# Sample sequences of an mLSTM: state products in bfloat16 parts on 32 columns each, state updates on 32 rows each, splits interleaved over states

## The chip, the core and the metric

The kernel runs on one core of a Trainium2 chip. TensorE multiplies matrices into PSUM, VectorE and ScalarE work on elements and move results out of PSUM, GpSimd does some element work and issues DMAs, SyncE (SP) issues most DMAs. Each engine works through its own instructions in order and waits on semaphores for the others. The metric is the device time of one execution in microseconds, the median of three runs.

## What is computed

One layer of a hybrid decoder: an input projection of 512 prompt tokens and 64 sample tokens (8 sequences of 8 tokens), an mLSTM with 4 heads of 256, a convolution module, an output projection and a layer norm. All is float32 to the tolerance of the reference. The change touches the samples in the mLSTM alone, which is, for each head and each of the 8 sequences with its own state C of 256 x 256 and n of 256:

```python
num = (w_inter[..., None] * jnp.einsum('bhtd,bhde->bhte', qc, C)
       + jnp.einsum('bhts,bhse->bhte', s, vc))
den = w_inter * jnp.einsum('bhtd,bhd->bht', qc, n) + jnp.sum(s, axis=-1)
h = num / jnp.maximum(jnp.abs(den), jnp.exp(-m_t))[..., None]
C_new = decay[..., None, None] * C + jnp.einsum('bhs,bhsd,bhse->bhde', ws, kc, vc)
```

## The kernel before

**Precision.** A float32 product is made of three products of parts: a value is split into hi (a rounded copy, by ScalarE) and lo (the rest, by VectorE), both float32r, and hi*hi + lo*hi + hi*lo is accumulated.

**The input projection** sets the pace. It has 64 column blocks; three are done first, the others are the stages of the loop over ORDER, from stage 4 on. A stage runs over 16 steps k (KT); a step is six matmuls L184, three pairs of 256 and 320 columns, into one of two PSUM tiles pp. The weights come in units of four steps: SP loads raw (two units each), `split` (L76) makes whi on ScalarE (L85) and wlo on VectorE (L86) and is called three units ahead (RING 4), so that whi of a unit waits until TensorE is done with the unit four before. At a stage's end `evac` moves pp out: for q, k, v two ScalarE passes; for o two sigmoid passes (L757) and a GpSimd product (L774); for zm two sigmoid passes, two VectorE passes (L763) and a GpSimd product (L778).

**All other work is placed beside it** by a table at the foot: `at(s, k, f, ...)` has f emitted right after step k of stage s. The order of emission is the order on each engine. For head h the sample work counts from o: stage 8, step 8 for head 0, and stage 6h+7, step 10 for the others (steps past 15 run on into the next stages). `at(o[0], o[1] + n, ...)` is n steps after that. Head 3's sample work lies beside stages with o and zm.

**The sample work of a head** was `b_sC`, called for each of 8 states b, four steps apart. Its first part adds q*C to one bank ns of 64 + 64 rows: QM holds the hi and lo parts of the weighted q of b in two places of a window of 128 columns, all else zero, so that each matmul L611 has 128 weight columns, and 258 columns of the state's hi (Chi, L380 on ScalarE) or lo (Clo, L381 on VectorE) stream through; with the first state the float32 product of Es and vs is added (L614, two matmuls on 64 rows and columns). Its second part, for odd b, updates two states: four matmuls L623 on 32 rows each (k times v of one sequence, 128 weight columns, 256 streamed), then L629 on VectorE (state times decay plus the product, in place in Ct), a GpSimd DMA of the new state (L630), and SP loads of two later states. `c_split` of a state is called one block ahead. `b_sLN` then evicts ns (L637), brings its lower half beside the upper by a DMA of ScalarE, adds, and normalises; `b_shT` transposes. The PSUM tiles mi (three banks in turn) serve all of this and the prompt's work, ns is one bank.

**Close to it:** `head_ln` of the prompt on VectorE and ScalarE at offset 7, its transposes `b_hT` at offsets 14 and 16 (evicted by L601), and the next head's parts: `b_parts` of q (ScalarE qh, VectorE ql), and `b_E` (ten exponentials and one of Es on ScalarE).

Of the kernel before, what the change touches and what calls it, by code (L numbers as in the profile page):

```python
# [55 lines left out]
def hybrid(ctx, tc, x0, wg0, wu, wgate, cpack, gpack, sct, hist, xres, lnp,  # L56
# [398 lines left out]
    def b_q(h):  # L455

        q, QM = KQV["q", h], m["QM"]
        qw = m["t"]([P, 2, TS], F32, "qw")
# [3 lines left out]
        act.activation(QM[:, :, 0:T8], qv, AF.Copy)  # L462
        dve.tensor_sub(QM[:, :, TS:TS + T8], qv, QM[:, :, 0:T8])
# [139 lines left out]
    def b_sC(h, b):  # L603
        if b == 0:
            m["ns"] = ns_tile()
        i = NB * h + b
        ch, cl = CH.pop(i)
        for d in range(2):
            w = m["QM"].rearrange("p a c -> p (a c)")[:, d * NB * P + b * 120:d * NB * P + b * 120 + P]
            for n, c in enumerate((ch, cl)):  # L610
                pe.matmul(m["ns"][:, :258], lhsT=w, rhs=c[:, d], start=b == 0 and d == 0 and n == 0,  # L611
                          stop=b == NB - 1 and d == 1 and n == 1)
            if b == 0 and d == 0:
                pe.matmul(m["ns"][:TS, :258], lhsT=m["Es"], rhs=m["vs"], start=False, stop=False)  # L614
        c_split(i + 1)
        if b % 2 == 0:
            return
        pss = []
        for bb in (b - 1, b):
            g, j = divmod(bb, 4)  # L620
            ps = mi((P, 2, DH))
            for d in range(2):
                pe.matmul(ps[:, d], lhsT=m["kS"][32 * j:32 * j + 32, g, d * P:(d + 1) * P],  # L623
                          rhs=m["vS"][32 * j:32 * j + 32, g], start=True, stop=True)
            pss.append(ps)
        for bb, ps in zip((b - 1, b), pss):
            ct = CS.pop(NB * h + bb)
            c = ct[:, :, :DH]
            dve.scalar_tensor_tensor(c, c, m["dec", h][:, bb:bb + 1], ps, op0=OP.mult, op1=OP.add)  # L629
            pool.dma_start(o_cs[NB * h + bb], c)  # L630
        c_load(i + 4)
        c_load(i + 5)

    def b_sLN(h, part):
        if part == 0:
            nsb, m["t2"] = m["t"]([P, 1, 258], F32, "nsb"), m["t"]([TS, 258], F32, "nsl")
            act.activation(nsb[:, 0], m["ns"][:, :258], AF.Copy)  # L637
            act.dma_start(m["t2"], nsb[TS:, 0])
            m["nsb"] = nsb
# [465 lines left out]
```

## Time and profile before

| | |
|---|---|
| median of 3 runs | 1145.18 us (1144.78 to 1145.86) |
| the profiled execution | 1145.27 us |
| its span, first to last instruction | 1143.3 us |
| TensorE busy | 1130.3 us, 99% of the span |
| VectorE busy | 722.0 us, 63% |
| ScalarE busy | 406.1 us, 36% |
| GpSimd busy | 147.0 us, 13% |

The profile is of one execution. Between the span and the time lie 2.0 us that no instruction covers. Busy times are sums over the span; a matmul's record covers its whole way through the array, so that matmuls overlap in the records and the distance from start to start tells what one costs. Where an engine idles, the profile names what released it.

### The profile page before, as it was taken

How to read it: one execution, taken by the hardware profiler on the slowest of the kernel's cores; microseconds unless marked ns; L12 is line 12 of the kernel's file. 1: busy time of each engine (PE TensorE's matmuls, PEld its weight loads, DVE VectorE, ACT ScalarE, POOL GpSimd, SP SyncE). 2: the span in 40 equal slices, each digit the busy share in tenths (PEclk: the TensorE clock that was granted, in tenths of full speed). 3: DMA queues.
4: the chain of work that ended last, by engine and by line, in shares of the span. 5: the costliest groups of instructions: out<-in, count | busy, mean ns of one | idle time of the engine just before them, and what ended most of it. 6: DMA issues, size and time to landing. Idle time of an engine off the chain costs nothing.

```text
span 1143.3 us, 19722 instructions
## 1 busy us (share of the span) xinstructions
PE 1130.3 (99%) x8062; PEld 1085.9 (95%) x8062; DVE 722.0 (63%) x1207; ACT 406.1 (36%) x772; POOL 147.0 (13%) x217
## 2 busy tenths in 40 slices
PE   9999999999999999999999999999999999999996
PEld 8999999999999999999999999999999988888895
DVE  6385455455355445428899998999977872433447
ACT  5335453345344443422222222222236651221224
POOL 0022030011002003101010111111203310000004
PEclk9999999999999999999999999999999999999998
DMA  8114262253245224222223222222222246632229
GB/s 292 68 57 132 77 195 86 77 185 96 74 134 168 67 74 160 86 87 90 93 92 108 87 100 85 85 81 75 93 93 75 92 145 188 205 143 93 70 87 166
DMA packets 43659, 127.50 MB, mean 112 GB/s; under 512 B 5372, under 2 KB 10108, under 8 KB 43120
## 3 DMA queue, kind: packets, MB, share of 16 engines
q1 hardware_dynamic: 37712, 112.44, 30.0%
q0 software_dynamic: 4992, 12.94, 4.3%
q8 instruction: 63, 1.03, 0.4%
q10 hardware_dynamic: 864, 0.85, 0.3%
q14 instruction: 28, 0.23, 0.1%
HBM read 110.11 MB, written 18.72 MB: 113 GB/s over the span
## 4 chain that ended last, share of the span: by engine, by line
PE 99%; DVE 1%; issue 0%; DVEq 0%
PE pp L184 71%; PE pp L977 3%; PE pp L978 3%; PE pp L979 3%; PE mi L978 2%; PE mi L979 2%; PE mi L977 2%; PE ns L611 1%; PE mi L442 1%; PE mi L974 1%; PE mi L973 1%; PE mi L549 1%; PE mi L184 1%; PE mi L557 1%; PE mi L623 1%; PE ns L979 0%
## 5 line engine op out<-in xcount | busy, mean ns | idle before, releaser
L184 PE MATMUL pp<-xh,whi 128*128 128x256 f32 (+1 forms) x1952 | 423.3, 298 | 0.0
L184 PE MATMUL pp<-xl,whi 128*128 128x256 f32 (+1 forms) x1952 | 416.5, 295 | 0.0
L184 PE MATMUL pp<-xh,wlo 128*128 128x256 f32 (+1 forms) x1952 | 415.5, 295 | 0.0
L86 DVE TENSOR_TENSOR wlo<-raw,whi 128x512 fp32r<-128x512 f32 x300 | 221.8, 742 | 266.9 <-ACT whi L85 266.5
L85 ACT ACTIVATE whi<-raw 128x512 fp32r<-128x512 f32 x300 | 188.5, 632 | 391.9 <-PE pp L184 246.1
L184 PEld LDWEIGHTS pp<-xh,wlo 128*128 128x128 f32 x1952 | 326.7, 188 | 0.0
L184 PEld LDWEIGHTS pp<-xl,whi 128*128 128x128 f32 x1952 | 326.4, 188 | 0.0
L184 PEld LDWEIGHTS pp<-xh,whi 128*128 128x128 f32 x1952 | 321.6, 189 | 3.0 <-issue 0.3
L724 DVE SCALAR_TENSOR_TENSOR Y<-U,cp,Y 128x512 f32<-128x512 f32 x240 | 189.8, 791 | 5.3
L978 PE MATMUL pp<-whi,mx 128*128 128x512 f32 (+1 forms) x128 | 46.9, 366 | 0.0
L977 PE MATMUL pp<-whi,mx 128*128 128x512 f32 (+1 forms) x128 | 46.9, 366 | 0.0
L979 PE MATMUL pp<-wlo,mx 128*128 128x512 f32 (+1 forms) x128 | 46.8, 366 | 0.0
L630 POOL DMA_DIRECT2D o_cs<-Ct x32 | 22.5, 717 | 181.9 <-DVE Ct L629 181.9
L381 DVE TENSOR_TENSOR Clo<-Ct,Chi 128x516 fp32r<-128x516 f32 x35 | 25.7, 733 | 27.4 <-ACT Chi L380 27.4
L757 ACT ACTIVATE sg<-pp,cp 128x256 f32<-128x256 f32 (+1 forms) x48 | 21.4, 496 | 45.4 <-PE pp L184 45.4
L978 PE MATMUL mi<-whi,mx 128*128 128x512 f32 (+1 forms) x96 | 36.1, 376 | 0.0
L977 PE MATMUL mi<-whi,mx 128*128 128x512 f32 (+1 forms) x96 | 36.0, 375 | 0.0
L979 PE MATMUL mi<-wlo,mx 128*128 128x512 f32 (+1 forms) x96 | 36.0, 375 | 0.0
L979 PEld LDWEIGHTS pp<-wlo,mx 128*128 128x128 f32 x128 | 24.1, 188 | 4.3
L977 PEld LDWEIGHTS pp<-whi,mx 128*128 128x128 f32 x128 | 24.1, 188 | 4.3
L978 PEld LDWEIGHTS pp<-whi,mx 128*128 128x128 f32 x128 | 24.0, 188 | 4.3
L1005 POOL DMA_DIRECT2D o_ys<-zs x4 | 3.4, 1184 | 188.9 <-ACT zs L1004 188.9
(334 smaller groups left out, 1370.1 us busy)
## 6 DMA issues: line engine op xcount, KB each, us to landing
raw<-wu SPq DMA_DIRECT2D x154, 512.0 KB, 3.3
Ct<-sct SPq DMA_DIRECT2D x32, 258.0 KB, 2.8
o_cs<-Ct POOLq DMA_DIRECT2D x32, 256.0 KB, 2.8
xr<-x SPq DMA_DIRECT2D x16, 288.0 KB, 5.0
z<-xres SPq DMA_DIRECT2D x8, 512.0 KB, 5.9
wr<-wg SPq DMA_DIRECT2D x16, 192.0 KB, 5.1
o_y<-z POOLq DMA_DIRECT2D x11, 256.0 KB, 7.6
o_y<-lnp SPq DMA_DIRECT2D x2, 1024.0 KB, 10.0
```

The costliest lines, as they stand in the source:

```text
L85: act.activation(hi, r, AF.Copy)
L86: (eng or dve).tensor_tensor(out=lo, in0=r, in1=hi, op=OP.subtract)
L184: pe.matmul(out[b], lhsT=w, rhs=x[:, slice(*SPANS[b])], start=k == 0 and n < 2, stop=k == KT - 1 and n >= 4)
L381: dve.tensor_sub(CH[i][1], CS[i], CH[i][0])
L442: pe.matmul(dst[J], lhsT=m[k_][:, d, J * P:(J + 1) * P], rhs=m[q_][:, d, J * P:S], start=d == 0 and n == 0, stop=d == 1 and n == 2)
L549: pe.matmul(ps[:, :258], lhsT=m[p_][:, o:o + P], rhs=m[v_][:, J], start=J == 0 and n == 0, stop=J == I and n == 2)
L630: pool.dma_start(o_cs[NB * h + bb], c)
L724: dve.scalar_tensor_tensor(y, u, w, y, op0=OP.mult, op1=OP.add)
L757: act.activation(sg[:, c0:c1], ps, AF.Sigmoid, bias=b_in[:, c:c + 1])
L977: pe.matmul(ps, lhsT=h_, rhs=hi, start=first, stop=False)
L978: pe.matmul(ps, lhsT=l_, rhs=hi, start=False, stop=False)
L979: pe.matmul(ps, lhsT=h_, rhs=lo, start=False, stop=last)
```

## The change

The state is split into three bfloat16 parts in place of two float32r parts, and so is q. Q holds 32 columns for each half d and sequence: 8 tokens of part 0, of part 1, of part 2, and 8 zeros. `b_qC` takes four sequences at a time (group r, states 4r to 4r+3): each has its own 32 columns of weights and so its own 32 rows of one mi bank, and 24 matmuls run over halves, state parts and sequences. All nine products of parts thus lie in the rows and are added later: the bank goes to nsb, after the second group a DMA of ScalarE writes both groups to DRAM (nsd), eight DMAs of SP bring them back with the three q parts side by side (n3), and `b_sLN` adds them to the product of Es and vs, which has its own bank and eviction now. `b_sKV` makes the updates of four states: eight matmuls on 32 rows each, over three mi banks and ns, ordered so that neighbours lie on different rows. `c_split` has two calls per state and interleaves neighbours: c0 of state j is made in the same call as c1 of state j-1, and cr (the state less c0) of j in the same call as c2 of j-1. Ct has 8 buffers instead of 5, loaded 8 ahead by `c_next`. c0 and c1 share memory with Ph and Pl.

```diff
-            CH[i] = [m["t"]([P, 2, 258], F32R, n, bufs=2) for n in ("Chi", "Clo")]
-            act.activation(CH[i][0], CS[i], AF.Copy)
-            dve.tensor_sub(CH[i][1], CS[i], CH[i][0])
+    def c_split(i, j, part):
+        if (j, part) == (0, 0):
+            for n, tag in (("c0", "Ph"), ("c1", "Pl"), ("c2", None)):
+                m[n] = m["t"]([P, 4, 2, 258], BF16, n, tag=tag)
+            m["cr"] = {}
...
+        if part == 0:
+            if j:
+                act.activation(c1[:, j - 1], cr[j - 1], AF.Copy)
+            if j < 4:
+                act.activation(c0[:, j], CS[i + j], AF.Copy)
+        else:
+            if j:
+                dve.tensor_sub(c2[:, j - 1], cr.pop(j - 1), c1[:, j - 1])
+            if j < 4:
+                cr[j] = m["t"]([P, 2, 258], F32, "cr", bufs=2)
+                dve.tensor_sub(cr[j], CS[i + j], c0[:, j])
...
-        act.activation(QM[:, :, 0:T8], qv, AF.Copy)
-        dve.tensor_sub(QM[:, :, TS:TS + T8], qv, QM[:, :, 0:T8])
+        act.activation(p_[0], qv, AF.Copy)
+        dve.tensor_sub(qv, qv, p_[0])
+        act.activation(p_[1], qv, AF.Copy)
+        dve.tensor_sub(p_[2], qv, p_[1])
...
-    def b_sC(h, b):
...
+    def b_qC(h, r):
+        if r == 0:
+            m["nsb"] = m["t"]([P, 2, 258], F32, "nsb")
+        ps = mi()
+        for d in range(2):
+            for n in ("c0", "c1", "c2"):
+                for j in range(4):
+                    pe.matmul(ps[32 * j:32 * j + 32, :258], lhsT=m["Q"][:, d, 4 * r + j], rhs=m[n][:, j, d],
+                              start=d == 0 and n == "c0", stop=d == 1 and n == "c2")
+        act.activation(m["nsb"][:, r], ps[:, :258], AF.Copy)
+        if r:
+            act.dma_start(nsd[h].rearrange("j i t r e -> (j i t) r e"), m["nsb"])
+
+    def b_sKV(h, r):
+        pss = [mi((P, 2, DH)) for _ in range(3)] + [ns_tile().rearrange("p (d e) -> p d e", d=2)]
+        for d in range(2):
+            for j in range(4):
+                rows = slice(32 * j, 32 * j + 32)
+                pe.matmul(pss[j][:, d], lhsT=m["kS"][rows, r, d * P:(d + 1) * P], rhs=m["vS"][rows, r],
+                          start=True, stop=True)
+        for j in range(4):
+            b = 4 * r + j
+            c = CS.pop(NB * h + b)[:, :, :DH]
+            dve.scalar_tensor_tensor(c, c, m["dec", h][:, b:b + 1], pss[j], op0=OP.mult, op1=OP.add)
+            pool.dma_start(o_cs[NB * h + b], c)
+
+    def c_next(h, r):
+        for j in range(4):
+            c_load(NB * (h + 1) + 4 * r + j)
...
-        at(o[0], o[1] + 5, c_split, NB * h)
-        for i in range(NB):
-            at(o[0], o[1] + 12 + 4 * i, b_sC, h, i)
-        at(o[0], o[1] + 42, b_sLN, h, 0)
-        at(o[0], o[1] + 48, b_sLN, h, 1)
-        at(o[0], o[1] + 66, b_shT, h)
+        for r in range(2):
+            for j in range(5):
+                for part in range(2):
+                    at(o[0], o[1] + (8, 26)[r] + 3 * j + 2 * part, c_split, NB * h + 4 * r, j, part)
+            at(o[0], o[1] + (22, 39)[r], b_sKV, h, r)
+            at(o[0], o[1] + (25, 43)[r], b_qC, h, r)
+            at(o[0], o[1] + (29, 50)[r], c_next, h, r)
+        at(o[0], o[1] + 26, b_sLN, h, 0)
+        at(o[0], o[1] + 49, b_sLN, h, 1)
+        at(o[0], o[1] + 64, b_sLN, h, 2)
+        at(o[0], o[1] + 74, b_shT, h)
```

The lines of the changed kernel: L395 and L393 are c0 and c1, L401 and L398 cr and c2, L634 the matmuls of b_qC, L646 and L651 those of b_sKV and the update, L86 and L87 the splits of the weights, L188 the projection, L793 the sigmoid passes.

VectorE, head 1, the second half of the sample work; c_3035, c_3036 and c_3037 are c0, c1 and c2. Before:

```order
L381 TENSOR_TENSOR Clo<-Ct,Chi 128x516 [waits DMAHW2_49,Activation_49]
L86 TENSOR_TENSOR wlo<-raw,whi 128x512 [waits PE_49,Activation_49]
L381 TENSOR_TENSOR Clo<-Ct,Chi 128x516 [waits DMAHW3_49,Activation_49]
L629 SCALAR_TENSOR_TENSOR Ct<-Ct,dec,mi 128x2x256 [waits DMASW1_49,PE_49]
L629 SCALAR_TENSOR_TENSOR Ct<-Ct,dec,mi 128x2x256 [waits DMASW2_49,DVE_49,PE_49]
```

Now:

```order
L401 TENSOR_TENSOR cr<-Ct,c_3035 128x516 [waits DMAHW1_49]
L87 TENSOR_TENSOR wlo<-raw,whi 128x512 [waits DMAHW5_49,PE_49,Activation_49]
L398 TENSOR_TENSOR c_3037<-cr,c_3036 128x516 [waits DVE_49]
L401 TENSOR_TENSOR cr<-Ct,c_3035 128x516 [waits DMAHW2_49]
L398 TENSOR_TENSOR c_3037<-cr,c_3036 128x516 [waits Activation_49]
L401 TENSOR_TENSOR cr<-Ct,c_3035 128x516 [waits DMAHW3_49,Activation_49]
L87 TENSOR_TENSOR wlo<-raw,whi 128x512 [waits PE_49,Activation_49]
L651 SCALAR_TENSOR_TENSOR Ct<-Ct,dec,mi 128x2x256 [waits DMASW6_49,PE_49]
L651 SCALAR_TENSOR_TENSOR Ct<-Ct,dec,mi 128x2x256 [waits DMASW7_49,PE_49]
L651 SCALAR_TENSOR_TENSOR Ct<-Ct,dec,mi 128x2x256 [waits DMASW0_49,PE_49]
L651 SCALAR_TENSOR_TENSOR Ct<-Ct,dec,ns 128x2x256 [waits DMASW1_49,DVE_49,PE_49]
L398 TENSOR_TENSOR c_3037<-cr,c_3036 128x516 [waits Activation_49]
```

The last c2 of the group stands behind all four updates, and a wlo stands between cr and c2 of a state.

ScalarE, head 3, the first half of the sample work, to the eviction of stage 26 (zm); c_5180 and c_5181 are c0 and c1. Before:

```order
L601 ACTIVATE hT_5139<-mi,cp 128x512 [waits PE_49]
L380 ACTIVATE Chi<-Ct 128x516
L85 ACTIVATE whi<-raw 128x512 [waits DMAHW5_49,PE_49]
L380 ACTIVATE Chi<-Ct 128x516 [waits DVE_49]
L757 ACT_TABLE_LOAD
L757 ACTIVATE sg<-pp,cp 128x256 [waits PE_49]
L757 ACTIVATE sg<-pp,cp 128x320
```

Now:

```order
L393 ACTIVATE c_5181<-cr 128x516 [waits DVE_49]
L395 ACTIVATE c_5180<-Ct 128x516 [waits DMAHW0_49]
L624 ACTIVATE hT_5279<-mi,cp 128x512 [waits PE_49]
L393 ACTIVATE c_5181<-cr 128x516 [waits DVE_49]
L395 ACTIVATE c_5180<-Ct 128x516 [waits DMAHW1_49]
L86 ACTIVATE whi<-raw 128x512 [waits DMAHW0_49,PE_49]
L393 ACTIVATE c_5181<-cr 128x516 [waits DVE_49]
L793 ACT_TABLE_LOAD
L793 ACTIVATE sg<-pp,cp 128x256 [waits PE_49]
L793 ACTIVATE sg<-pp,cp 128x320
```

The table load and the sigmoid passes stand behind c1 of the fourth state, which waits for VectorE's cr.

TensorE, head 1: before, the last block of the sample work.

```order
L611 MATMUL ns<-Chi,QM 128x258 [waits Activation_49]
L611 MATMUL ns<-Clo,QM 128x258 [waits DVE_49]
L611 MATMUL ns<-Chi,QM 128x258
L611 MATMUL ns<-Clo,QM 128x258
L623 MATMUL mi<-vS,kS 128x256 [waits PE_49]
```

Now, a piece of the second b_qC, with the first half's c1 and c2:

```order
L634 MATMUL mi<-c_3036,Q 32x258 [waits Activation_49]
L634 LDWEIGHTS Q
L634 MATMUL mi<-c_3037,Q 32x258
...
L634 MATMUL mi<-c_3037,Q 32x258 [waits DVE_49]
L634 LDWEIGHTS Q
L634 MATMUL mi<-c_3035,Q 32x258
```

The fourth of the c2 matmuls waits for VectorE's last c2, with the whole second half d behind it.

## Rows read from the trace of the kernel before

**Rows 1.** The page's part 4: shares of the chain that ended last.

```profile
PE 99%; DVE 1%; issue 0%; DVEq 0%
```

**Rows 2.** Timeline of TensorE, head 1's last block: start, duration (us), engine, line.

```profile
253.82 0.28 PE L611 MATMUL ns<-Chi,QM 128*128 128x258 f32 x1
...
254.18 0.28 PE L611 MATMUL ns<-Clo,QM 128*128 128x258 f32 x1
254.39 0.50 PE L623 MATMUL mi<-vS,kS 32*128 32x256 f32 x4
254.82 0.53 PE L184 MATMUL pp<-xh,whi 128*128 128x256 f32 x2
255.19 0.43 PE L184 MATMUL pp<-xl,whi 128*128 128x256 f32 x2
...
257.31 0.43 PE L184 MATMUL pp<-xh,whi 128*128 128x256 f32 x2
```

**Rows 3.** Timeline of TensorE, head 0's first block, from its first to the next.

```profile
136.92 0.28 PE L611 MATMUL ns<-Chi,QM 128*128 128x258 f32 x1
...
138.17 0.43 PE L184 MATMUL pp<-xh,whi 128*128 128x256 f32 x2
```

**Rows 4.** Timeline of TensorE, the first 7 us of the span.

```profile
1.53 3.59 PE L219 MATMUL ns<-warm 128*128 128x512 bf16 x8 [1.53 <-DVE warm L216]
...
5.88 0.68 PE L184 MATMUL mi<-xh,wh 128*128 128x256 f32 x2
6.36 0.81 PE L184 MATMUL pp<-xl,wh 128*128 128x256 f32 x4
```

**Rows 5.** Timelines of ScalarE and VectorE, 157 to 163 us, head 0.

```profile
157.26 0.63 ACT L85 ACTIVATE whi<-raw 128x512 fp32r<-128x512 f32 x1 [2.51 <-PE pp L184]
157.80 0.62 ACT L380 ACTIVATE Chi<-Ct 128x516 fp32r<-128x516 f32 x1
...
161.56 0.63 ACT L85 ACTIVATE whi<-raw 128x512 fp32r<-128x512 f32 x1
...
162.22 0.69 DVE L86 TENSOR_TENSOR wlo<-raw,whi 128x512 fp32r<-128x512 f32 x1 [1.58 <-ACT whi L85]
162.83 0.69 DVE L381 TENSOR_TENSOR Clo<-Ct,Chi 128x516 fp32r<-128x516 f32 x1
```

**Rows 6.** Timelines of VectorE, ScalarE and GpSimd, 423 to 439 us, head 3.

```profile
423.81 0.68 DVE L86 TENSOR_TENSOR wlo<-raw,whi 128x512 fp32r<-128x512 f32 x1
...
430.71 1.28 ACT L757 ACT_TABLE_LOAD   x1
433.44 0.89 ACT L757 ACTIVATE sg<-pp,cp 128x256 f32<-128x256 f32 x2 [1.45 <-PE pp L184]
...
434.37 0.94 DVE L763 SCALAR_TENSOR_TENSOR sg<-pp,cp,sg 128x256 f32<-128x256 f32 x2 [2.01 <-ACT sg L757]
...
435.82 1.91 DVE L381 TENSOR_TENSOR Clo<-Ct,Chi 128x516 fp32r<-128x516 f32 x1
437.66 1.40 DVE L629 SCALAR_TENSOR_TENSOR Ct<-Ct,dec,mi 128x512 f32<-128x512 f32 x2
...
435.46 1.72 POOL L778 TENSOR_TENSOR hT<-hT,sg 128x576 f32<-128x576 f32 x1 [3.27 <-DVE sg L763]
```

**Rows 7.** Timelines of VectorE and ScalarE, 222 to 229 us, head 1.

```profile
222.59 0.69 DVE L86 TENSOR_TENSOR wlo<-raw,whi 128x512 fp32r<-128x512 f32 x1
...
228.17 0.69 ACT L601 ACTIVATE hT<-mi,cp 128x512 f32<-128x512 f32 x1 [0.88 <-PE mi L598]
```

**Rows 8.** Timeline of TensorE, the matmuls after offset 43 of heads 0 and 3.

```profile
169.57 0.43 PE L184 MATMUL pp<-xh,whi 128*128 128x256 f32 x2
...
455.01 0.43 PE L184 MATMUL pp<-xh,whi 128*128 128x256 f32 x2
```

**Rows 9.** The last matmul, and busy time by engine, PEclk, DMA of a window.

```profile
1131.63 0.28 PE L979 MATMUL pp<-lastl,mx 128*128 128x256 f32 x1
...
1136.00:1144.00 8.00, 0.00 (x0) 0.00 (x0) 3.10 (x4) 0.00 (x0) 0.00 (x0) 0.53 0.67 201
```

More of the change, by code (lines that the diff above doesn't have):

```diff
@@ L9 @@
 F32R = mybir.dt.float32r
+BF16 = mybir.dt.bfloat16
 AF = mybir.ActivationFunctionType
@@ L213, in g0_load @@
             nc.sync.dma_start(wr[k], wg0[k])
-    warm = g0t([P, 512], mybir.dt.bfloat16, "warm")
+    warm = g0t([P, 512], BF16, "warm")
     dve.memset(warm, 1.0)
@@ L392, in open_m @@
         m["vs"] = t([TS, 258], F32, "vs")
-        m["QM"] = t([P, 2 * NB, P], F32R, "QM")
+        m["Q"] = t([P, 2, NB, 32], BF16, "Q")
         pool.memset(m["vs"][:, 256:257], 1.0)
         pool.memset(m["vs"][:, 257:258], 0.0)
-        pool.memset(m["QM"].bitcast(F32), 0.0)
+        pool.memset(m["Q"], 0.0)
         rb_load(0)
-        for i in range(5):
+        for i in range(8):
             c_load(i)
@@ L461, in b_q @@
         qv = qw.rearrange("p d (b t) -> p (d b) t", t=T8)
[L462 to L463 removed]
+        p_ = [Q.rearrange("p d b c -> p (d b) c")[:, :, i * T8:(i + 1) * T8] for i in range(3)]
+        act.activation(p_[0], qv, AF.Copy)
+        dve.tensor_sub(qv, qv, p_[0])
+        act.activation(p_[1], qv, AF.Copy)
+        dve.tensor_sub(p_[2], qv, p_[1])
     def b_kT(h, a):
@@ L601, in b_hT @@
         act.activation(hT[e][:, :S], ps, AF.Copy, scale=hn_g[:, e:e + 1])
-    def b_sC(h, b):
[L604 to L607, printed above, removed]
-        for d in range(2):
[L609 to L632, printed above, removed]
@@ L634, in b_sLN @@
+    def c_next(h, r):
+        for j in range(4):
+            c_load(NB * (h + 1) + 4 * r + j)
     def b_sLN(h, part):
         if part == 0:
[L636 to L639, printed above, removed]
-        else:
-            nums = m["nums"] = m["nsb"][:TS]
-            dve.tensor_add(nums[:, 0], nums[:, 0], m["t2"])
+            ps = mi()
+            pe.matmul(ps[:TS, :258], lhsT=m["Es"], rhs=m["vs"], start=True, stop=True)
+            m["nums"] = m["t"]([TS, 1, 258], F32, "nums")
+            act.activation(m["nums"][:, 0], ps[:TS, :258], AF.Copy)
+        elif part == 1:
+            m["n3"] = m["t"]([TS, 3, 258], F32, "n3", tag="nsb")
+            for r in range(2):
+                for j in range(4):
+                    b = 4 * r + j
+                    nc.sync.dma_start(m["n3"][b * T8:(b + 1) * T8], nsd[h][j, :3, :, r].rearrange("i t e -> t i e"))
+        else:
+            nums = m["nums"]
+            for i in range(3):
+                dve.tensor_add(nums[:, 0], nums[:, 0], m["n3"][:, i])
@@ L694, in hybrid @@
         at(o[0], o[1] + 16, b_hT, h, 1)
-        at(o[0], o[1] + 5, c_split, NB * h)
-        for i in range(NB):
-            at(o[0], o[1] + 12 + 4 * i, b_sC, h, i)
-        at(o[0], o[1] + 42, b_sLN, h, 0)
-        at(o[0], o[1] + 48, b_sLN, h, 1)
-        at(o[0], o[1] + 66, b_shT, h)
+        for r in range(2):
+            for j in range(5):
[8 more added lines that the diff above has]
+        at(o[0], o[1] + 74, b_shT, h)
     cv = {}
```

19 lines of the change are left out of this document (11 added, 8 removed).

## The prediction

> **What bounds the kernel now.** I read the page's chain first: 99% of the chain of work that ended last is TensorE's own [rows 1]. So each microsecond of matmul taken out of the stretch from 137 to 455 us, where the four heads' sample work lies, is a microsecond off the end, as long as nothing makes TensorE wait. Then I read TensorE's timeline around the sample work, because busy times of pipelined matmuls overlap and only starts tell what one costs. One pair of projection matmuls takes 0.265 us ((257.31 - 255.19) / 8), so one step k of the inner loop, three pairs, takes 0.80 us; a matmul of 258 columns takes 0.12 [rows 2]. Below, "offset n" is the n that the table at the foot adds to o[1]; one offset is one step. Last I read ScalarE's and VectorE's timelines in the same places. They are half idle, but their idle time is not free to use: their work comes in order, and links that wait for each other run at the pace of the links.
>
> **What is removed on TensorE.** A block of an odd state holds four matmuls L611 and four L623. It runs from 253.82 to 254.82, 1.00, and the next pair takes 0.37 in place of 0.265, so 1.11 [rows 2]. A block of an even state is four L611, 0.48. The first block of a head also holds the two L614 and runs from 136.92 to 138.17, 1.25 [rows 3]; without its four L611, L614 with its switches is 0.77. A head is 4 x 1.11 + 3 x 0.48 + 1.25 = 7.1 us, four heads 28.5.
>
> **What is put in its place on TensorE.** (a) b_sKV, twice a head, eight matmuls on 32 rows. Four took 0.43 (254.39 to 254.82) plus 0.09 before and 0.11 after for the switch, 0.63 in all [rows 2]. If eight over four row groups run in the time of four, 0.63; if they scale, 1.06. I take the middle, 0.85. (b) b_qC, twice a head, 24 matmuls of 258 columns on 32 columns each. Eight bfloat16 matmuls of 512 columns took 3.59 us in the first stretch, at the lower clock, 0.45 each, about twice what 512 columns cost at 0.12 for 258 [rows 4]; so I price a bfloat16 column like a float32r one. No row shows column groups side by side. If four run in the time of one, 6 x 0.12 plus 0.2 for the switch is 0.9; if one after another, 24 x 0.12 + 0.2 = 3.1. The nearest row, four L623 on separate row groups, shows them in 0.43, which decides neither; I take 1.1, because the four matmuls of a group have their own rows of the output and share nothing but the stream. (c) The matmul of Es alone, 0.77. A head is 2 x 0.85 + 2 x 1.1 + 0.77 = 4.7, so 2.4 saved, 10 us over four heads, if TensorE never waits. (The Trainium skill, TensorE: Matmul & The Clock Gate, section "Part 3: Packing small matmuls", gives three column tiles a speedup of 2.38. By that (b) would be an estimated 2.9 / 2.38 + 0.2 = 1.4 and the saving 8. No run here shows it yet.)
>
> **What is added on ScalarE and VectorE.** A state had one pass on each, L380 and L381; it has two on each now: c0 (ScalarE), cr (VectorE), c1 (ScalarE), c2 (VectorE), each needing the one before it. A pass follows another on its own engine after 0.53 (ScalarE, 157.26 to 157.80) or 0.60 (VectorE, 162.22 to 162.83), and a pass starts 0.03 after the end of a 0.63 or 0.69 pass on the other engine [rows 5]. I take bfloat16 outputs at the same price; no row shows them. The order of both engines (the fences in the section on the change) puts whi and wlo of a weight unit between the links of three of the four states. Per state the chain is then cr 0.72, c1 0.53, the next c0 0.53, whi 0.66, wlo 0.60, c2 0.60 = 3.64 us, and without a weight unit 0.72 + 0.65 + 0.60 = 1.97. The table gives 3 steps, 2.4 us. So the chain falls behind, and TensorE stands at the last part of b_qC.
>
> Where c2 of the fourth state is ready, head 1, second group. TensorE passes the end of offset 43 at 257.31 today [rows 2]. Without the 7.1, with the first group's b_sKV and b_qC, Es and the wait of 0.5 below, it ends the Es matmul at 257.31 - 7.1 - 17 x 0.80 + 0.85 + 0.5 + 1.1 + 0.77 = 239.8. ScalarE can then evict it (0.3), make qh twice, and VectorE ql twice, before the first cr: 2.15 us, 242.0. Then two states at 3.64, one at 1.97: the fourth cr at 251.2. wlo, held by whi behind two evictions of the stage, comes 1.25 later, four state updates L629 at 0.66 (437.66, two in 1.40 [rows 6]) come in front of c2, and c2 takes 0.69: 251.2 + 1.85 + 2.64 + 0.69 = 256.4. TensorE reaches that matmul at about 239.8 + 13.6 + 0.85 + 0.5 = 254.7. It waits 1.7 us, and after c2 it has 13 of the 24 matmuls left, 0.75. It passes offset 43 at 257.2: nothing is left of the 2.4. Head 2 has the same order, so the same.
>
> Head 1, first group. VectorE is free of the head norm and one wlo at 223.2 [rows 7]; cr, c1, c0 follow, hT's eviction (228.17 less the 1.25 that TensorE has been spared) pushes the second c1 to 227.5, and the fourth cr stands at 232.5, its c1 ends at 233.8, two evictions, whi, wlo and c2 end at 236.4, and the first L629 ends at 237.1. b_qC's bank is the one it frees, and TensorE is there at 236.6: a wait of 0.5, which is in the sum above.
>
> Head 0. The same sum puts TensorE at b_qC of the second group at 166.0 and back at 169.57 today [rows 8]. Here the exponentials of the next head's E stand between the second c0 and the third c1 on ScalarE, 3.24 us (157.80 + 0.53 to 161.56 [rows 5]), so the fourth c2 ends at about 168.3: a wait of 1.8, the end at 169.1, a gain of 0.5.
>
> Head 3. Two things are in the way. ScalarE's table load for the sigmoid, 1.28, ran at 430.71, early and for nothing, and the sigmoid passes began at 433.44 when the stage's matmuls ended [rows 6]. Now the load stands behind c1 of the fourth state, which waits for its cr. By the same links from 423.3 (423.81 [rows 6] less the pass L380 that stood ahead of the norm) the fourth cr is at 431.7, c1 ends at 433.0, the sigmoid begins at 434.3. From there to the first L629 it took 4.22 (433.44 to 437.66), because gating passes and a VectorE pass of 1.91 beside GpSimd's 1.72 stand in between [rows 6]. So the first bank is free at 434.3 + 4.2 + 0.74 = 439.3, while TensorE is there at 434.3: a wait of 4.9. The second group starts that much later, again with a GpSimd product beside it, and its c2 ends at about 457.5; offset 43 is passed at 458.3, today at 455.01 [rows 8]: 3.3 us lost.
>
> Small edits. The weights' splits have three units (9.6 us) of lead and the lag stays under 4, so no projection waits. On SP the c_next loads stand ahead of weight loads and wait for o_cs, eight offsets after the updates; today they wait in the same place. The 32 small loads of n3 wait for one DMA of ScalarE that has six offsets, 4.8 us, to land, and are read 15 offsets after that: nothing. Two more adds in b_sLN are beside matmuls. The smaller memset and the three further loads of open_m are far ahead of need.
>
> **Sum.** -0.5 + 0 + 0 + 3.3 = +2.8 on the profiled execution's 1145.27, which lies 0.09 above the median of 1145.18; on the median, 1148.0. In words: 10 us of matmuls saved, 13 us of waits put in.
>
> **The rivals.**
> 1. The splits keep up (faster). It needs the second group's chain 1.8 us shorter in heads 0 to 2 and head 3's first group 4.9 shorter; bfloat16 passes that run well under 0.53 and 0.60 would do it, since 16 of them lie in a group. For it: both engines are half idle, and each wait is only a small part of a chain of 17 us. Against: every link was taken from rows. All of it gives 1145 - 10 = 1135; half of it 1140.
> 2. The clock falls. TensorE idles 4.9 us in head 3. The only fall in this trace comes in the window 1136 to 1144, whose mean is 0.53, that is at about 1136.4, 4.5 us after the last matmul ended (1131.63 + 0.28) [rows 9]. So the level of 2.4 GHz would go to 1.2 just as TensorE goes on. In the first stretch a pair still took 0.48 at 5.88, 4.3 us after the first matmul at 1.53 [rows 4]; some 5 us at that pace lose 2.5, of which the second group's wait of 1 hides its part: +1.5, 1149.5. (The Trainium skill, same page, section "Part 1: The HAM clock gate", has the clock gated back to half after idling; the last row here agrees, at its 4.5 us. By that rule the time is the 1149.5.)
> 3. Column groups one after another: b_qC is 3.1 instead of 1.1. The first one moves the second group's chain by 2.0, and after c2 1.8 in place of 0.75 are left: +3 a head, 1160.
> 4. The waits are there but smaller, above all head 3's, if the sigmoid's load runs earlier than its place in the order: 1145.
>
> **How the numbers follow.** Forecast as summed 0.40, rival 1 0.20, rival 2 0.17, rival 3 0.08, rival 4 0.15. A measurement tells about 0.2%, 2.3 us, from no change: 1142.9 to 1147.5. Faster is rival 1, 0.20. Same is rival 4 and the low side of the forecast (a link's error of 0.05 over the 14 or so links of a chain is 0.7 a head), 0.23. Slower is the rest, 0.57. The range leaves out rival 3 and the fuller half of rival 1: 1141 to 1153, the upper end for rival 2 with longer links.
>
> **What would show it.** Right: TensorE idle before L634 in all heads, released by VectorE (c2 or Ct), 1.5 to 2 us in the second groups and near 5 in head 3's first; L634's 24 matmuls in about 1 us where they don't wait; DVE busy up by some 20 us. Wrong: no idle time before L634 (rival 1), 24 matmuls over 2.5 us (rival 3), or a slice with a clock under 1.00 near 440 us (rival 2). A wait before L188 would mean that the weights' splits lost their lead, which I ruled out.

## The result and the profile after

The changed kernel takes 1150.95 us, the median of 4 runs (1149.99 to 1151.97), against 1145.30 for the kernel before (1144.78 to 1145.86): a ratio of 1.0051, interval 1.0038 to 1.0063. That is 5.65 us slower, where 2.8 were forecast (1148.0, range 1141 to 1153). The profiled execution took 1150.39 us with a span of 1148.7, against 1145.27 and 1143.3 before: 5.1 us.

The page's part 4, the shares of the chain that ended last (it answers to [rows 1]), and the view of TensorE's waits (total us, times, longest), both of after:

```profile
PE 93%; DVE 4%; ACT 2%; issue 1%; DVEq 0%; ACTq 0%
```

```profile
PE mi L634 <- DVE c L398: 6.4, 4, 1.8
PE mi L634 <- DVE Ct L651: 5.7, 3, 4.9
```

The chain has left TensorE for 6% of the span, to VectorE and ScalarE. TensorE stands 12.1 us ahead of L634, the matmul of `b_qC`, and at nothing else behind the first stretch: four times for c2 (L398), three times for the bank that the first update L651 frees. Those are the two waits that the prediction named. One by one, from the same trace, against the forecast:

| wait ahead of L634 | forecast us | after us |
|---|---|---|
| head 0, second group | 1.8 | 1.70 |
| heads 1 and 2, first group, each | 0.5 | 0.42 |
| heads 1 and 2, second group, each | 1.7 | 1.82 |
| head 3, first group | 4.9 | 4.87 |
| head 3, second group | 1.0 | 1.05 |
| sum | 12.1 | 12.1 |

(The prediction's sum in words says 13 us of waits; its seven waits add up to 12.1.) One of them in TensorE's timeline, head 1's second group, where [rows 2] has the last old block (start, duration in us, engine, line; in brackets the idle time and its releaser):

```profile
253.52 0.51 PE L634 MATMUL mi<-c,Q 128*32 128x258 bf16 x11
255.85 0.60 PE L634 MATMUL mi<-c,Q 128*32 128x258 bf16 x13 [1.82 <-DVE c L398]
256.38 0.38 PE L188 MATMUL pp<-xh,whi 128*128 128x256 f32 x1
```

Eleven of the 24 matmuls go, then the twelfth waits for c2 of the fourth state. The projection goes on at 256.38. In head 3 the chain reads as forecast (ScalarE, VectorE, TensorE; it answers to [rows 6]):

```profile
433.51 0.63 ACT L393 ACTIVATE c<-cr 128x516 bf16<-128x516 f32 x1 [1.97 <-DVE cr L401]
434.16 1.28 ACT L793 ACT_TABLE_LOAD   x1
435.46 0.89 ACT L793 ACTIVATE sg<-pp,cp 128x256 f32<-128x256 f32 x2
...
436.38 0.94 DVE L799 SCALAR_TENSOR_TENSOR sg<-pp,cp,sg 128x256 f32<-128x256 f32 x2 [2.90 <-ACT sg L793]
...
437.84 1.89 DVE L398 TENSOR_TENSOR c<-cr,c 128x516 bf16<-128x516 f32 x1
439.65 2.05 DVE L651 SCALAR_TENSOR_TENSOR Ct<-Ct,dec,mi 128x512 f32<-128x512 f32 x3
...
440.44 1.48 PE L634 MATMUL mi<-c,Q 128*32 128x258 bf16 x24 [4.87 <-DVE Ct L651]
```

The last c1 waits for cr, the table load stands behind it, then come the sigmoid, the gating passes, c2 (1.89 us long beside GpSimd's product), the first update, and only then has `b_qC` a bank. The last line shows something more: the 24 matmuls take 1.48 us here. The windows of after tell why (us, busy PE with its count, granted clock, DMA share, GB/s):

```profile
350.00:354.00 4.00, 2.89 (x30) 1.00 0.35 132
354.00:358.00 4.00, 3.29 (x23) 0.59 0.91 324
358.00:362.00 4.00, 4.00 (x31) 0.98 0.31 91
436.00:440.00 4.00, 0.00 (x0) 1.00 0.27 79
440.00:444.00 4.00, 3.56 (x32) 0.57 0.58 203
```

The granted clock falls from 1.00 to a mean of 0.57 in the 4 us behind head 3's wait. With only the two levels of 2.4 and 1.2 GHz, that is 3.4 us at the lower one (0.43 x 4 x 2), 0.4 of it still inside the wait (the mean from 440.00 to 440.44 is 0.59 already), so that it costs 1.5. It falls once more at the end of head 2's 1.82 us wait (0.59 and 0.98: again 3.4 us, here all of it with TensorE at work, which costs 1.7), and not behind the equal waits of heads 0 and 1. The prediction had the first fall as rival 2 and not the second.

One thing is in neither trace's waits. Position by position in the projection, after loses 2.8 us against before between the 3000th matmul into pp (517.3 us in before) and 860 us, where no sample work is left, and wins 3.7 in the output projection. The experiments begin with that.

### The profile page after: what moved, and what is told of

Same layout as the page of the kernel before. It is cut to its first block, busy times and chain, and to the rows that moved or that the text cites. A ratio compares the mean times of both kernels' runs of the same rounds, so it can differ in the third digit from the quotient of the medians.

```text
span 1148.7 us, 19950 instructions
## 1 busy us (share of the span) xinstructions
PE 1123.7 (98%) x8126; PEld 1080.2 (94%) x8126; DVE 741.1 (65%) x1248; ACT 423.8 (37%) x813; POOL 144.8 (13%) x217
## 4 chain that ended last, share of the span: by engine, by line
PE 93%; DVE 4%; ACT 2%; issue 1%; DVEq 0%; ACTq 0%
PE pp L188 67%; PE pp L1015 3%; PE pp L1014 3%; PE pp L1013 3%; PE mi L1014 2%; PE mi L1015 2%; PE mi L1013 2%; PE mi L462 1%; PE mi L1010 1%; PE mi L1009 1%; PE mi L572 1%; PE mi L188 1%; DVE Ct L651 1%; PE mi L580 1%; DVE c L398 1%
## 5 line engine op out<-in xcount | busy, mean ns | idle before, releaser
L188 PE MATMUL pp<-xh,whi 128*128 128x256 f32 (+1 forms) x1952 | 426.7, 300 | 0.0
L188 PE MATMUL pp<-xl,whi 128*128 128x256 f32 (+1 forms) x1952 | 419.7, 297 | 0.0
L188 PE MATMUL pp<-xh,wlo 128*128 128x256 f32 (+1 forms) x1952 | 419.4, 297 | 0.0
L87 DVE TENSOR_TENSOR wlo<-raw,whi 128x512 fp32r<-128x512 f32 x300 | 218.3, 731 | 271.2 <-ACT whi L86 269.7
L188 PEld LDWEIGHTS pp<-xh,whi 128*128 128x128 f32 x1952 | 326.7, 190 | 5.5 <-issue 4.0
L188 PEld LDWEIGHTS pp<-xl,whi 128*128 128x128 f32 x1952 | 330.1, 190 | 0.0
L188 PEld LDWEIGHTS pp<-xh,wlo 128*128 128x128 f32 x1952 | 330.0, 190 | 0.0
L86 ACT ACTIVATE whi<-raw 128x512 fp32r<-128x512 f32 x300 | 187.2, 629 | 341.2 <-PE pp L188 198.3
L1014 PE MATMUL pp<-whi,mx 128*128 128x512 f32 (+1 forms) x128 | 46.4, 363 | 0.0
L793 ACT ACTIVATE sg<-pp,cp 128x256 f32<-128x256 f32 (+1 forms) x48 | 21.3, 495 | 45.1 <-PE pp L188 45.0
L1014 PE MATMUL mi<-whi,mx 128*128 128x512 f32 (+1 forms) x96 | 35.7, 371 | 0.0
L393 ACT ACTIVATE c<-cr 128x516 bf16<-128x516 f32 x32 | 20.2, 630 | 28.6 <-DVE cr L401 28.6
L398 DVE TENSOR_TENSOR c<-cr,c 128x516 bf16<-128x516 f32 x32 | 23.3, 729 | 8.9 <-ACT c L393 8.7
L1014 PEld LDWEIGHTS pp<-whi,mx 128*128 128x128 f32 x128 | 24.2, 189 | 3.7
```

The costliest lines, as they stand in the source:

```text
L86: act.activation(hi, r, AF.Copy)
L87: (eng or dve).tensor_tensor(out=lo, in0=r, in1=hi, op=OP.subtract)
L188: pe.matmul(out[b], lhsT=w, rhs=x[:, slice(*SPANS[b])], start=k == 0 and n < 2, stop=k == KT - 1 and n >= 4)
L393: act.activation(c1[:, j - 1], cr[j - 1], AF.Copy)
L398: dve.tensor_sub(c2[:, j - 1], cr.pop(j - 1), c1[:, j - 1])
L793: act.activation(sg[:, c0:c1], ps, AF.Sigmoid, bias=b_in[:, c:c + 1])
```

## The experiments

**1. The places of two small tiles.** The kernel before, with nothing but this part of the diff:

```diff
-    bmask = mt([P, 4, 4], F32, "bmask")
...
+        consts["bmask"] = bmask = g0t([P, 4, 4], F32, "bmask")
...
-        s2 = mt([P, 2, 4], F32, "s2")
+        s2 = g0t([P, 2, 4], F32, "s2")
```

> The kernel before, with nothing changed but the place of two small constant tiles (bmask and s2), which the change moved out of the main pool into the gates' pool; the tiles behind them in the main pool lie at other addresses. Why: in the trace of after, one projection matmul follows another after 133.3 ns from the first stages to the end, in the trace of before after 132.2 ns until 854 us and after 133.3 only behind that; over some 5500 matmuls this is about 6 us that the prediction did not have, while the output projection at the end is 3.7 us shorter in after. Theory A (the addresses set the pace): 133.3 ns from the start, about 6 us lost by 850 us, some 3.7 won at the end, the time 1147 to 1148. Theory B (the pace comes from elsewhere: the chip, the chance of a run, or the new instructions): 132.2 ns as in before, the time within 0.1% of before, 1144.5 to 1146.

Measured: 1147.24 (10 runs, 1146.68 to 1147.51) against 1145.16 for the kernel before beside it, ratio 1.0017 (1.0008 to 1.0026). The projection's pace is 133.3 ns from the first stages on, as in after; 5.4 us are lost by 859 us and 3.7 come back in the output projection. Theory A holds. So 2.1 of the 5.65 us have nothing to do with the products: they come with two constants that left the main pool.

**2. All waits taken away.** The changed kernel with other offsets in the table (head: splits, updates, products, next loads, Es, small loads):

```diff
+    PLAN = {0: ((8, 26), (22, 39), (25, 45), (29, 50), 26, 50)}
+    PLAN[1] = PLAN[2] = (8, 27), (22, 40), (26, 47), (30, 51), 27, 53
+    PLAN[3] = (8, 33), (22, 46), (32, 53), (36, 57), 27, 59
...
```

> The changed kernel with other offsets in the table alone: the last group products come 2 offsets later in head 0, 4 later in heads 1 and 2 (first group 1 later), 7 and 10 later in head 3. Theory A (the saved matmul time was given back in waits for the splits and for the updates that stand ahead of them on VectorE, and in two falls of the clock): the 12.1 us of idle time before L634 go, the clock stays at 1.0, which gives back 3.4 more; 1150.4 - 12.1 - 3.4 = 1134.9, between 1133 and 1138. Theory B (the waits move to another place as the chains are in arrears all through the stage): the idle time stands before L634 again or before the next head's products, and the time stays over 1143. Theory C (the switches between tile sizes or the pace of the projection cost the time): the waits go but the time stays over 1140.

Measured: 1139.76, ratio 0.9955 (0.9938 to 0.9971). No wait of L634 is left, but one that I had not thought of stands in head 3: the Es matmul, still at offset 27, needs a bank too.

```profile
PE mi L661 <- DVE Ct L651: 3.3, 1, 3.3
```

Behind it the clock falls for 3.4 us. With that wait and that fall, 5.0 us, the time is what A said plus them. Moving Es to offset 33 in head 3 tests it:

```diff
-    PLAN[3] = (8, 33), (22, 46), (32, 53), (36, 57), 27, 59
+    PLAN[3] = (8, 33), (22, 46), (32, 53), (36, 57), 33, 59
```

> As e2_later, with the Es matmul of head 3 (L661) behind the group products too, at offset 33 in place of 27. In e2_later it stood 3.3 us, for the bank that the first update L651 frees, and the clock fell right then for 3.4 us. Theory A (that bank was the last cause of waits): no wait of TensorE behind the first 10 us, the clock 1.0 to the end of the matmuls, 1139.76 - 3.3 - 1.7 = 1134.8. Theory B (the chain behind head 3's updates moves on and some other user of a bank stands): 1137 to 1140.

Measured: 1134.55, ratio 0.9910 (0.9893 to 0.9926); no wait behind the first 10 us, the clock 1.0 to the end of the matmuls. Theory A to 0.25 us. Against e1_layout, which has the old products and the same places of tiles, the new products are worth 12.7 us once nothing waits for them. Position by position the two traces are 12.1 us apart at the 3000th matmul into pp, where the sample work is done, and the same 12.1 at the last matmul: all of it lies in the sample work.

**3. Head 3 alone.** Only head 3's row of e2's table, heads 0 to 2 as in after.

```diff
...
+    PLAN[1] = PLAN[2] = (8, 26), (22, 39), (25, 43), (29, 50), 26, 49
+    PLAN[3] = (8, 33), (22, 46), (32, 53), (36, 57), 27, 59
```

> The changed kernel with the later offsets of e2_later in head 3 alone; heads 0 to 2 as in after. Theory A (each wait is a loss of its own): the waits of 4.87 and 1.05 us of head 3 and one fall of the clock (1.7 us) go, those of heads 0 to 2 (1.70, 0.42, 1.82, 0.42, 1.82) stay: 1150.4 - 7.6 = 1142.8. Theory B (head 3's wait absorbs delay that shows up somewhere else once it is gone, or the sigmoid's table load still holds it): 1147 to 1150.4.

Measured: 1149.22, only 1.7 better than after: near B by its number, and in part for B's reason: Es took over 3.3 of head 3's 5.9 us of waits. The waits of heads 0 to 2 were those of after (1.70, 0.42, 1.82, 0.42, 1.83). The rest is the clock, three falls in place of two; it fell behind the second-group waits of heads 0 and 1 this time, and not in head 2 (columns as in the windows above; the third row is head 2, the last head 3):

```profile
169.00:173.00 4.00, 4.00 (x16) 0.57 0.85 290
...
258.00:262.00 4.00, 4.00 (x23) 0.57 0.70 244
...
354.00:358.00 4.00, 2.17 (x28) 1.00 0.56 194
...
442.00:446.00 4.00, 3.88 (x15) 0.57 0.59 200
```

**4. Column groups in another order.** As e2_later, with the loops of `b_qC` turned round:

```diff
-            for n in ("c0", "c1", "c2"):
-                for j in range(4):
+        for j in range(4):
+            for d in range(2):
+                for n in ("c0", "c1", "c2"):
```

> As e2_later, with the loops of the group products turned round: all six products of one state, then the next state, so that matmuls on the same 32 columns follow each other, in place of four states in turn. Theory A (four column groups run side by side only because neighbours in the order have different columns): 24 matmuls at some 0.12 us each, 2.9 us a group in place of 0.8, eight groups: 2.1 x 8 = 17 us over e2_later, near 1152. Theory B (matmuls that follow each other on one column group cost no more): the same time as e2_later within 2 us.

Measured: 1144.50 in one run, 4.7 over the median of e2_later and 5.5 over its profiled execution: neither theory. TensorE's timeline, head 1's second group, of this kernel and then of e5_es_later, which has the order of after and no wait:

```profile
255.98 0.43 PE L188 MATMUL pp<-xh,wlo 128*128 128x256 f32 x2
256.34 1.54 PE L634 MATMUL mi<-c,Q 128*32 128x258 bf16 x24
257.81 0.54 PE L188 MATMUL pp<-xh,whi 128*128 128x256 f32 x2
258.18 0.43 PE L188 MATMUL pp<-xl,whi 128*128 128x256 f32 x2
```

```profile
254.39 0.42 PE L188 MATMUL pp<-xh,wlo 128*128 128x256 f32 x2
254.74 0.85 PE L634 MATMUL mi<-c,Q 128*32 128x258 bf16 x24
255.52 0.53 PE L188 MATMUL pp<-xh,whi 128*128 128x256 f32 x2
255.89 0.43 PE L188 MATMUL pp<-xl,whi 128*128 128x256 f32 x2
```

From the start of the pair ahead to the start of the second pair behind, less the two pairs (0.53), the group costs 0.97 us with four column groups in turn (255.89 - 254.39 - 0.53) and 1.67 with one state after the other (258.18 - 255.98 - 0.53). Eight groups at 0.70 more are 5.6, which is the difference of the profiled executions. In turn, four matmuls start within 15 ns and the next four 0.1 us later: they run side by side. State by state, part of that is still there, since 24 one after another would be 2.9; why it is about half, these runs don't tell.

**5. The updates ahead of c2.** One offset of after changed, in heads 1 and 2:

```diff
-            at(o[0], o[1] + (22, 39)[r], b_sKV, h, r)
+            at(o[0], o[1] + (22, 41 if h in (1, 2) else 39)[r], b_sKV, h, r)
```

> The changed kernel with one offset changed: b_sKV of the second group of heads 1 and 2 at 41 in place of 39, so that its four updates L651 (0.66 us each on VectorE) stand behind the last c2 and no longer in front of it. Theory A (the prediction's chain: the updates put 2.6 us into the way of c2): c2 is there 2.6 us earlier, the wait of 1.82 us in heads 1 and 2 goes, or leaves 0.3 for the bank of the first update; two heads 3.6 us, with the fall of the clock in head 2, where it occurs, up to 1.7 more: 1147.4 or 1145.7. Theory B (c2 is late because of its own chain cr, c1, c2 and the weights' passes): the waits stay within 0.5 us of 1.82 and the time at 1150.5 to 1151.

Measured: 1148.04, with a wide spread, 1145.06 to 1149.44 in 10 runs. The mechanism is A's: the second-group waits of heads 1 and 2 shrink from 1.82 to 0.29 each, and what is left is the bank.

```profile
254.37 0.84 PE L634 MATMUL mi<-c,Q 128*32 128x258 bf16 x24 [0.29 <-DVE Ct L651]
```

By the end of head 2 this trace is 4.5 us ahead of after's (two waits and the fall in head 2). Then head 3's wait, unchanged at 4.9, brought a longer fall:

```profile
430.00:434.00 4.00, 1.07 (x9) 1.00 0.00 0
434.00:439.00 5.00, 3.04 (x30) 0.52 0.60 197
439.00:444.00 5.00, 5.00 (x19) 0.50 0.35 117
444.00:448.00 4.00, 4.00 (x30) 0.95 0.30 110
```

0.48 x 5 x 2 + 5 + 0.05 x 4 x 2 is 10.2 us at the lower level in place of 3.4. The wait ends at 435.96 and the mean clock from 434.00 to there is 0.55, so that 1.8 of the 10.2 lie inside the wait, and the fall costs 4.2. The spread of the ten runs goes with the clock: its mean over the run is 0.995 in the fastest (1145.06), 0.990 in the four slowest (1148.58 to 1149.44), which is some 11 us more at the lower level. So how long or how often the clock falls differs between runs of one kernel; only one run has a trace that tells where.

**6. The change at the old places.** After, with bmask and s2 in the main pool again (the diff of experiment 1 undone).

> The changed kernel with bmask and s2 in the main pool, as in the kernel before; nothing else. What is left between it and the kernel before is what the prediction summed: matmuls saved, waits put in, falls of the clock. Theory A (2.1 us of the 5.7 belong to the places of the tiles): 1150.95 - 2.1 = 1148.9, the waits before L634 as in after (12.1 us). Theory B (the places cost nothing here): 1151.

Measured: 1149.19, ratio to before 1.0037 (1.0023 to 1.0050). The number is near theory A's 1148.9, but by luck. The place is worth more to the new products than the 2.1 that A took (4.1 in experiment 7, e5_es_later less e6_es_later_old_places), the waits are a tenth of a us longer, 12.7 in all, and the clock fell in all four heads, two falls more than in after:

```profile
168.00:172.00 4.00, 4.00 (x16) 0.57 0.73 267
...
256.00:260.00 4.00, 4.00 (x30) 0.61 0.75 263
...
355.00:359.00 4.00, 3.29 (x23) 0.61 0.93 329
...
441.00:445.00 4.00, 3.91 (x33) 0.57 0.60 209
```

**7. Which place is it?** The kernel without waits at three more places. First at the old ones:

> As e5_es_later, with bmask and s2 in the main pool again, as in the kernel before: the rings of whi and wlo, the mix tiles and all of the later pools lie 96 bytes higher. e1_layout showed that moving these two tiles alone costs 2.1 us. Theory A (the addresses set the pace, whatever the schedule): projection matmuls at 132.2 ns up to 850 us, an output projection about 3.3 us longer than in e5_es_later, in sum 2.1 us less: 1132.7. Theory B (a tie of chance with the old schedule): the time of e5_es_later.

Measured: 1130.49, ratio 0.9873 (0.9859 to 0.9888): A in sign, and twice its size. The pace was 131.7 ns here, below the 132.2 of before, and it stayed there to the end of the projection; in before it rises to 133.3 at 860 us. The same window of 160 us in both traces, before first, one of the three kinds of projection matmul (count; ns min/median/max; first and last start):

```profile
L184 PE MATMUL pp<-xl,whi x404: 280/294/309, 559.8 to 719.9; 128*128 128x320 f32 x68, 128*128 128x256 f32 x67
```

```profile
L189 PE MATMUL pp<-xl,whi x406: 277/294/310, 560.2 to 719.9; 128*128 128x256 f32 x68, 128*128 128x320 f32 x68
```

All three kinds are 1212 and 1217. Nothing but the projection runs on TensorE there, and as built the two kernels differ in the addresses of the samples' own pool alone, which is closed by then. So a part of the pace, some 0.5 ns a matmul here, is not a matter of the tiles' places; from the 3000th matmul into pp to the end of the projection it makes 2.2 us. What it comes from, these runs don't show. Then one tile back at a time:

```diff
+    bmask = mt([P, 4, 4], F32, "bmask")
...
-        consts["bmask"] = bmask = g0t([P, 4, 4], F32, "bmask")
...
```

> As e5_es_later (1134.55), with bmask (64 bytes) in the main pool again and s2 (32 bytes) not. In the built program the rings of whi and wlo, which TensorE reads in the projection and in the output projection, start at byte 135040 of a partition in e5_es_later, 135104 here, 135136 in e6_es_later_old_places (1130.49). Theory A (what counts is where the rings stand against multiples of 64 bytes; here they stand on one, as in e5): projection matmuls every 133.3 ns, the output projection the short one, 1134.0 to 1135.2. Theory B (multiples of 128, or another tile, decide): a pace of 132.2 or less, 1130 to 1132.5.

```diff
-        s2 = g0t([P, 2, 4], F32, "s2")
+        s2 = mt([P, 2, 4], F32, "s2")
```

> As e5_es_later, with s2 (32 bytes) in the main pool again and bmask not: the rings start at byte 135072, 32 bytes off a multiple of 64, as in e6_es_later_old_places, but 64 bytes lower. Theory A (the rings against multiples of 64 bytes): the pace of e6, 131.7 to 132.2 ns, the output projection the longer one, 1130 to 1131.6. Theory B (multiples of 128, or another tile): 133.3 ns and 1134 to 1135.2.

Measured: 1126.72 (0.9839, 0.9823 to 0.9856) and 1140.89 (0.9964, 0.9951 to 0.9977). My rule of 64 bytes is wrong on both sides: e7 stands on a multiple of 64 and is the fastest of all, e8 does not and is the slowest of the kernels without waits. One kind of projection matmul in the same window, 560 to 720 us, of after, e7 and e8:

```profile
L188 PE MATMUL pp<-xl,whi x402: 281/297/312, 559.9 to 720.0; 128*128 128x256 f32 x67, 128*128 128x320 f32 x67
```

```profile
L189 PE MATMUL pp<-xl,whi x406: 280/294/310, 559.9 to 719.5; 128*128 128x256 f32 x68, 128*128 128x320 f32 x68
```

```profile
L188 PE MATMUL pp<-xl,whi x398: 280/298/315, 560.1 to 719.6; 128*128 128x256 f32 x199
```

All three kinds are 1203, 1218 and 1194 in the same time: from start to start 133.3, 131.7 and 134.2 ns. The difference is the same at each matmul, no single stop. Is it the rings, or the tiles ahead of them? 64 unused bytes right ahead of the rings decide:

```diff
+        if n == 0:
+            pool.memset(mt([P, 16], F32, "pad"), 0.0)
         if n < NU:
             WHI[n] = mt([P, 512], F32R, "whi", bufs=RING)
```

> As e5_es_later (1134.55), with 64 unused bytes in the main pool right ahead of the rings of whi and wlo. The rings start at byte 135104 as in e7_only_bmask_back (1126.72), and the pools of the later stages behind them lie where they lie there; the constants, the raw weights, hT and the tiles of q, k, v stay where they are in e5. Theory A (the place of the rings, which TensorE reads at every matmul of the projection and of the output projection, sets the pace): 1126.5 to 1127.5, projection matmuls every 131.7 ns. Theory B (the tiles ahead of the rings do): 1134 to 1135.2 at 133.3 ns.

Measured: 1127.06, ratio 0.9840 (0.9826 to 0.9855), pace 131.7 ns: theory A. Constants, raw weights, hT and the tiles of q, k, v stayed where they were. What moved is the rings and the pools behind them, and in the window above TensorE reads the rings and the unmoved x tiles alone. (That the moved tiles of the other engines have a part in it is not excluded.)

Last, the old products at the best of these places:

> The kernel before with s2 alone moved out of the main pool, so that the rings start at byte 135104 as in e7_only_bmask_back. It gives the old products at the best of the four places. Theory A (places and products add): e1_layout against e5_es_later differ by 12.7 us, the kernel before against e6_es_later_old_places by 14.7, so 1126.7 + 12.7 to 14.7 = 1139.4 to 1141.4. Theory B (each schedule has its own good place): 1143 or more.

Measured: 1139.50, ratio 0.9952 (0.9935 to 0.9969): at the low end of theory A, so places and products add here, 12.8 for the products as against 12.7 at after's place. At the place of before they are 14.6 (before less e6_es_later_old_places), 2 us more, of which the pace shown above makes 2.2. The medians side by side, in us (the kernel before took 1145.1 to 1145.3 beside each of them):

| rings start at byte | old products | after's offsets | later offsets, no waits |
|---|---|---|---|
| 135136 (as before) | 1145.2 | 1149.2 (e9) | 1130.5 (e6) |
| 135040 (as after) | 1147.2 (e1) | 1150.95 (after) | 1134.6 (e5) |
| 135104 | 1139.5 (e12) | not run | 1126.7 (e7), 1127.1 (e11) |
| 135072 | not run | not run | 1140.9 (e8) |

The best kernel, e7_only_bmask_back, is 1.6% faster than before.

**The ledger.** A time is that of the kernel without waits at the same place, plus its waits, plus half of the time that TensorE works at the lower clock. On the profiled executions (waits and falls from the views above):

| kernel | over e5 or e6 | waits | lower clock / 2 | sum |
|---|---|---|---|---|
| after | 15.8 | 12.1 | 1.7 + 1.5 | 15.3 |
| e2_later | 4.5 | 3.3 | 1.7 | 5.0 |
| e4_head3_later | 14.7 | 9.5 | 3 x 1.7 | 14.6 |
| e9_after_old_places | 19.2 | 12.7 | 4 x 1.7 | 19.5 |
| e10_updates_behind_c2 | 13.6 | 9.0 | 4.2 | 13.2 |

All five close within 0.6 us. So after against before is +2.1 (places), -12.7 (products), +12.1 (waits), +3.2 (falls of the clock): +4.7 of the 5.1 on the profiled executions. Taken the other way round, products first at the old place, it is -14.6 and then +4.1 for the places: the split between these two holds to 2 us, their sum is the same.

## Why the prediction was right, and where it was wrong

**What bounds the kernel, and the waits: right.** Each of the seven waits came within 0.2 us of its forecast, at the matmul named, with the releaser named, from durations of the trace of before and the order of the instructions alone. The chain through head 3 (c1, table load, sigmoid, gating, c2, first update, bank) stands in after as it was written; its sigmoid began at 435.46 in place of 434.3, but TensorE came later too, at 435.57 in place of 434.3. e10 confirmed the 2.64 us of updates ahead of c2, and e5 that without these waits nothing else stands. The sum of the waits is 12.1 in the prediction's own terms and in the trace.

**bfloat16 passes at the float32r price: right.** The passes of the split in after, on ScalarE (c1) and VectorE (c2), with busy us and mean ns:

```profile
L393 ACT ACTIVATE c<-cr 128x516 bf16<-128x516 f32 x32 | 20.2, 630 | 28.6 <-DVE cr L401 28.6
L398 DVE TENSOR_TENSOR c<-cr,c 128x516 bf16<-128x516 f32 x32 | 23.3, 729 | 8.9 <-ACT c L393 8.7
```

630 and 729 ns, against the 0.62 and 0.69 of single passes in [rows 5] (the mean of 729 holds the long one of 1.89). VectorE's busy time rose by 19 us (722.0 to 741.1), 20 forecast. Rival 1 fell with that.

**TensorE's saving: right in kind, sized too small.** What was mis-sized is the price of the new work, 4.7 us a head. `b_sKV` and Es in after:

```profile
249.34 0.43 PE L188 MATMUL pp<-xh,wlo 128*128 128x256 f32 x2
249.70 0.39 PE L646 MATMUL mi<-vS,kS 32*128 32x256 f32 x3
...
250.13 0.53 PE L188 MATMUL pp<-xh,whi 128*128 128x256 f32 x2
250.50 0.43 PE L188 MATMUL pp<-xl,whi 128*128 128x256 f32 x2
```

```profile
238.18 0.42 PE L188 MATMUL pp<-xh,wlo 128*128 128x256 f32 x2
238.53 0.65 PE L661 MATMUL mi<-vs,Es 64*64 64x258 f32 x2
239.11 0.54 PE L188 MATMUL pp<-xh,whi 128*128 128x256 f32 x2
239.48 0.43 PE L188 MATMUL pp<-xl,whi 128*128 128x256 f32 x2
```

Counted as the prediction counted the old blocks, with the slower first pair behind (two pairs off, 0.53), `b_sKV` is 0.63 (250.50 - 249.34 - 0.53) where I took 0.85, the middle of 0.63 and 1.06; Es is 0.77 (239.48 - 238.18 - 0.53) as forecast; `b_qC` is 0.97 (experiment 4) where I had 1.1. A head is 2 x 0.63 + 2 x 0.97 + 0.77 = 4.0 in place of 4.7, and four heads save 28.5 - 15.9 = 12.6. The kernels without waits show 12.7 and 12.8 at two places, so the account closes. Eight matmuls on four row groups cost what I had for four: the lower bound was the row to trust. (The Trainium skill, TensorE: Matmul & The Clock Gate, section "Part 3: Packing small matmuls", gives three column tiles a speedup of 2.38, from which the prediction made an estimated 1.4 for `b_qC`; the row says 0.97, and it decides.) Rival 3, column groups one after another, fell.

**The clock: the rival came, and more of it.** I had one fall, in head 3, at 0.17, for a net 1.5. After has two, e9 four. What I had read from [rows 9], a fall 4.5 us after the last matmul, made me take only head 3's wait for long enough. Head 3's fall did cost the 1.5 net, but by chance: it lasted 3.4 us and not some 5, and the second group's wait, 1.05, hid nothing of it. (The Trainium skill, same page, section "Part 1: The HAM clock gate", has the clock gated to half after idling; here the granted clock is 0.57 behind head 3's wait, and that waits under 2 us already bring a fall, in some cases, is this case's own.) The two falls add 3.2 in after, more than the whole miss of 2.85 (5.65 against 2.8).

**"Small edits": wrong by a thing that I did not price at all.** The prediction listed the moved constants' memset as far ahead of need, and I did not ask what else lies at another address when two tiles leave the pool. It cost 2.1 us in the old schedule. In this kernel the choice of place is worth more than the change: 14 us between e7 and e8.

**So the verdict was right and the number near in part by luck.** Within the sample work the sum should have read -12.7 + 12.1, no change; falls of the clock and the places of the tiles, 5.3 together, made it slower. Two terms that the sum had at nothing (3.2 and 2.1) and one that it had some 3 us too small (the saving) partly cancelled. Rival 4's smaller waits did not come.

## What to carry to other kernels

When work leaves the engine that bounds, ask when the results of the new, longer chain on the other engines are ready, by the order of their instructions, and put the consumer behind that time: the same products cost 5.65 us at one set of offsets and win 10.6 at another. Check every user of the same banks when a group of updates holds them, not only the one that waits today. Before a difference of some tenths of a per cent is put down to an edit, run the old kernel with the edit's tile addresses alone.

## What the runs showed of the hardware

- **The place of the weight rings (whi, wlo) in SBUF shifts TensorE's pace.** A shift of 32 bytes, from 135072 to 135104, changes a projection matmul from 134.2 to 131.7 ns, steadily, all through the projection. It is not the place alone: with all tiles in use at the same bytes, before ran at 132.2 and e6_es_later_old_places at 131.7. The output projection has its own preference: its matmuls L1014 into the mi banks took 371 ns in after (rows below, of the pages), and 376 in e6_es_later_old_places (L1019, the same statement), whose projection is the faster one (131.7 against 133.3). Which rule decides is open; multiples of 64 do not.

```profile
L1014 PE MATMUL mi<-whi,mx 128*128 128x512 f32 (+1 forms) x96 | 35.7, 371 | 0.0
```

```profile
L1019 PE MATMUL mi<-whi,mx 128*128 128x512 f32 (+1 forms) x96 | 36.1, 376 | 0.0
```

- **The clock falls behind short waits, by chance as far as these runs tell.** Of ten waits of 1.70 to 1.94 us (after, e4, e9, e10), six were followed by a fall, and the same wait of the same kernel form in head 2 had one in after and none in e4. All six waits of 3.29 us or more (e2 and e3 too) had one; the waits of 1.10 or less had none. A fall lasted 3.4 us in all cases but one, 10.2 in e10.
- **Four column groups of 32 run side by side**: 24 matmuls of 258 bfloat16 columns cost 0.97 us, switches included. With the order turned to one column group at a time it is 1.67.
